# A hybrid retention and attention layer: four orders and one queue changed in its second half

## The chip, the cores and the metric

The kernel runs on one core of one Trainium2 chip, as one launch. The metric is the device time of one execution in microseconds (us). TensorE (PE) multiplies matrices; VectorE (DVE), ScalarE (ACT) and GpSimd (POOL) do elementwise work; transfers are issued by SyncE (SP) or by ScalarE's own queue (ACTq).

## What is computed

One layer over 2048 tokens of width 1024, with 256 context tokens. A modulated RMS norm feeds one projection (3328 columns). Its columns serve two head groups: bidirectional retention (4 heads of 128, chunks of 128 tokens) and windowed attention (8 query heads of 64 on 2 key heads, blocks of 128 tokens, a sink logit, all context keys). Both are gated, joined, projected, added to the input and normed. Cut to what matters here:

```
def step(R, inp):                                   # retention, one chunk of 128 tokens
    qc, kc, vc = inp
    s = jnp.einsum('bhid,bhjd->bhij', qc, kc) * decay_in
    inner = jnp.einsum('bhij,bhje->bhie', s, vc)
    cross = jnp.einsum('bhid,bhde->bhie', qc, R) * decay_q
    R = R * decay_c + jnp.einsum('bhjd,bhje->bhde', kc * decay_k, vc)
    return R, inner + cross
...
y = out_f + jnp.flip(out_b, 2)
y = (y - mu) * lax.rsqrt(var + EPS)                 # per head and token
ret_x = merge_heads(y) * gn_w * jax.nn.silu(g)
...
p = jnp.exp(logits - m); p = p / (jnp.sum(p) + jnp.exp(sink - m))    # attention, 3 blocks + context
att_x = merge_heads(p @ v) * jax.nn.silu(ag)
x = x + gate * (concat([ret_x, att_x]) @ w_out)
return rms_norm(x) * final_norm_w
```

## The kernel before, in words

The first half (to about 677 us) projects all tokens, group by group of 512 tokens (`g` = 3, 2, 1, 0), and stores queries, keys, values, gates and chunk states to DRAM scratch. `do_gate` (L588) applies SiLU to a gate column block and stores it (L595); for the attention gates (`which` = 1) of groups 0 and 1 the store is issued by SP, for all others by ACT. The last attention-gate column block, for group 0, is interleaved on PE with the attention scores of token block 0: `WEAVE` (L35) says after which contraction step `k` of the two column blocks which jobs go. Digits are score heads 0 to 7; `s` is the first block's retention scores and decayed queries; `y` is its retention values, their moments, norm and rows, and its state update (L1127 to L1136).

The second half loops over 16 token blocks `b`, two steps each: `kv` = 0 and 1. In a step, `STEPS[kv]` (L29) lists the order of the calls. `a` is one score head of the next step (`att_head`, L725: four score matmuls into a single buffer S, a DVE operation L749 that adds the mask and takes the maximum, Exp on ACT). `N` divides that head by its sum (`att_norm`, L761: a DVE reciprocal L764 and a POOL scaling L765). `T` transposes one key tile of the four normalised heads on PE (L1155) and splits the result into a high part (ACT, L1157) and a low part (DVE, L1158); `V` multiplies both parts with the values (L1168), one after the other. `o` are pieces of the output projection (L1205). `q` makes the decayed queries of the next block (`ret_queries`, L773: two POOL products, L780), `S` its retention scores, `R` its values (L795 to L799), `B` and `r` its moments, norm and rows (L806 to L821; L814 waits for POOL's inverse root L118), `Y` transposes the rows and makes the gated retention input (L1191, L109, L1194). `U` updates the retention state by four DVE operations (`ret_state`, L823, L828) and issues the load of the next block's states (L686). The tile of decayed queries has one buffer, that of the loaded states two.

The calls are made in this order, but a planner places each instruction on its engine's queue: it goes by the order of the calls and by modelled times, and lets a later instruction that is ready fill a gap. `tc.issue_after(i)` (also as `behind(i)`, L217) makes an instruction stand behind `i` on its engine; it adds an order, no wait on another engine. Each queue then runs in order: an instruction that waits holds up all behind it, and a transfer that waits on SP holds up the transfers behind it.

`last` (L1232) ends the kernel: for each half row, the last output pieces, the addition, a sum of squares on ACT (L1241); then POOL adds the two sums (L1242), adds EPS (L117) and takes the inverse root (L118); then DVE scales both halves (L1245), and SP and ACT store one each.

Of the kernel before, what the change touches and what calls it, by code (L numbers as in the profile page):

```python
# [8 lines left out]
F32 = mybir.dt.float32  # L9
F32R = mybir.dt.float32r  # L10
BF16 = mybir.dt.bfloat16
AF = mybir.ActivationFunctionType
ALU = mybir.AluOpType
# [3 lines left out]
P = 128  # L17
# [6 lines left out]
RH = 4  # L24
AH = 8
EPS = 1e-6
# [5 lines left out]
)  # L32
FIRST = "T0 Y T1 V0 T2 V1 q T3 V2 T4 G V3 S V4"

WEAVE = ("00 21 42 63", "04s 25 46 67y")  # L35
CHUNKS = ["rk0", "rv0", "rk1", "rv1", "rq0", "rq1", "kv", "aq0", "aq1", "rg0", "rg1", "ag0", "ag1"]


# [1 line left out]
def tile_hymba(  # L40
# [17 lines left out]
    nc = tc.nc  # L58
    act, dve, pool, pe = nc.scalar, nc.vector, nc.gpsimd, nc.tensor
# [28 lines left out]
    gC = const.tile([P, 8], F32, name="gC")  # L88
# [4 lines left out]
    half4 = const.tile([P, 4], F32, name="half4")  # L93
# [21 lines left out]
    def inv_sqrt(dst, src, eps):  # L115

        pool.tensor_scalar(dst, src, EPSV[eps], 0.0, op0=ALU.add, op1=ALU.add)  # L117
        pool.tensor_tensor(dst, dst, half4[:, 0 : dst.shape[-1]], op=ALU.pow)  # L118
        return dst
# [10 lines left out]
    def tmp(name, shape=(P, GT), dt=F32):  # L130
        return tp.tile(list(shape), dt, tag="t", name=name)
# [18 lines left out]
    PE = {}  # L150
# [66 lines left out]
    def behind(i):  # L217
        return tc.issue_after(i.ins) if i else nullcontext()
# [369 lines left out]
    def do_gate(which, idx, g, ps, pin=False, t=None):  # L588

        t = tmp(f"g{which}{idx}{g}") if t is None else t  # L590
        i = act.activation(t, ps, AF.Silu)
        if pin:
            tc.keep_in_program_order(i)

        (nc.sync if which and g < 2 else act).dma_start(  # L595
            d_g[4 * g : 4 * g + 4, :, which, idx, :].rearrange("b d t -> d b t"),
            t.rearrange("d (b t) -> d b t", b=4),
        )
# [51 lines left out]
    C2 = {}  # L650

    def window(b):
        slots = sorted((x % 3, x) for x in (b - 1, b, b + 1) if 0 <= x < NB)
        return slots, [x - b + 1 for _, x in slots]
# [8 lines left out]
    VW, QKV, ST, AQ, GR, GA, XB, MR, MA, PB, RF, RT = ({} for _ in range(12))  # L663
# [97 lines left out]
    def att_norm(b, kv, j):  # L761
        n = len(window(b)[0]) * P + CTX
        pb, m4 = PB[(b, kv)]
        dve.reciprocal(m4[:, 2, j : j + 1], m4[:, 2, j : j + 1])  # L764
        pool.tensor_scalar(pb[:, j, 0:n], pb[:, j, 0:n], m4[:, 2, j : j + 1], 0.0, op0=ALU.mult, op1=ALU.add)  # L765

    BANKS = {"o": 1, "z": 2, "t": 3}

    def bank(name, tag="t", shape=(P, RH, P)):
        return (pwr if tag == "o" else pw).tile(list(shape), F32, tag=tag, name=name, bufs=BANKS[tag])  # L770


    def ret_queries(b):  # L773
        if b:
            RT[b] = (
                s1.tile([P, 2, RH, P], F32, tag="qd", name=f"qd{b}", bufs=1),
                s2.tile([P, RH, P], F32, tag="sd", name=f"sd{b}", bufs=1),
            )
        for dr in range(2):
            pool.tensor_tensor(RT[b][0][:, dr], QKV[b][:, 0], C2["decq"][:, dr], op=ALU.mult)  # L780

    def ret_scores(b):
        q, kT = QKV[b][:, 0], QKV[b][:, 1]
# [39 lines left out]
    def ret_state(b):  # L823

        rf, st = RF[b], ST[b]
        nf = st[:, 0] if b else rf
        for h in range(RH):
            dve.scalar_tensor_tensor(  # L828
                nf[:, h], rf[:, h], gC[:, h : h + 1], st[:, 0, h], op0=ALU.mult, op1=ALU.add
            )  # L830
        RF[b + 1] = nf

    def tables():
# [46 lines left out]
    def unit(name, g, w):  # L880
        kind, idx = name[:2], int(name[-1]) if name[-1].isdigit() else 0
        if g == "c":
            {"rk": lambda: ctx_rk(idx, w), "rv": lambda: ctx_rv(idx, w), "kv": lambda: ctx_kv(w)}[kind]()
        elif kind == "rv":
            do_rv(idx, g, w)
        elif kind == "kv":
            do_kv(g, w)
        elif kind in ("rg", "ag"):
            for c in range(2):
                ps = cols_by_tok(w, c * P, H[g], GT, f"{name}{g}{c}")  # L890
                flush()
                do_gate(0 if kind == "rg" else 1, 2 * idx + c, g, ps)
        else:
            finish(name, g, [cols_by_tok(w, c * P, H[g], GT, f"{name}{g}{c}") for c in range(2)])
# [104 lines left out]
    for c in range(4):  # L999
        do_gate(0, c, 3, first[(f"rg{c // 2}", c % 2)])  # L1000
# [27 lines left out]
    for c, ps in enumerate(tiles):  # L1028
        do_gate(0, c, 2, ps)
# [93 lines left out]
    def head(i):  # L1123
        att_head(0, i // 4, i % 4)
        att_norm(0, i // 4, i % 4)
# [7 lines left out]
    ps = []  # L1133
    for c, weave in enumerate(WEAVE):
        at = {int(w[0]): [jobs[x] for x in w[1:]] for w in weave.split()}
# [9 lines left out]
    s2 = ctx.enter_context(tc.tile_pool(name="s2", bufs=2, reuse_waits="tile"))  # L1145
    pw = ctx.enter_context(tc.tile_pool(name="pw", bufs=1, space=PSUM, reuse_waits="tile"))
    fw, vctx = C2["fw"], C2["vctx"]
# [3 lines left out]
    def att_t(b, kv, kt):  # L1151
        pb = PB[(b, kv)][0]
        ppt = bank(f"pt{b}_{kv}_{kt}")
        for j in range(4):
            pe.transpose(ppt[:, j], pb[:, j, kt * P : (kt + 1) * P], ident)  # L1155
        phl = s2.tile([P, 2, 4, P], F32R, tag="phl", name=f"phl{b}_{kv}_{kt}", bufs=2)
        PE["phl"] = act.activation(phl[:, 0], ppt, AF.Copy)  # L1157
        dve.tensor_tensor(phl[:, 1], ppt, phl[:, 0], op=ALU.subtract)  # L1158
        PH[kt] = phl

    def att_v(b, kv, kt):
# [37 lines left out]
    def proj(b, n2, k):  # L1199
        if k == 0:  # L1200
            PZ[n2] = bank(f"pz{b}_{n2}", "z", (P, GT))
        m = (MR if k < RH else MA)[b]
        s = slice(n2 * GT, (n2 + 1) * GT)
        for i, (a, c) in enumerate(PASSES):
            pe.matmul(  # L1205
                PZ[n2], m[:, a, k % RH, :], WG[k // 4][c][:, k % 4, s],
                start=(k == 0 and i == 0), stop=(k == NK - 1 and i == 2),
            )
        if k == NK - 1:
            dve.tensor_tensor(XB[b][:, s], PZ[n2], XB[b][:, s], op=ALU.add)  # L1210
# [21 lines left out]
    def last(b):  # L1232

        xb = XB[b]
        ss = s2.tile([P, 2], F32, tag="sl", name="sl")
        junk = s1.tile([P, D], F32, tag="junk", name="junkl", bufs=1)
        hs = [slice(n * GT, (n + 1) * GT) for n in range(2)]
        for n in range(2):
            for i in range(4):
                proj(b, n, 4 + i)  # L1240
            act.activation(junk[:, hs[n]], xb[:, hs[n]], AF.Square, scale=1.0 / 32, accum_out=ss[:, n : n + 1])  # L1241
        pool.tensor_tensor(ss[:, 0:1], ss[:, 0:1], ss[:, 1:2], op=ALU.add)  # L1242
        rz = inv_sqrt(s2.tile([P, 1], F32, tag="rz", name="rzl"), ss[:, 0:1], 0)
        for n in range(2):
            dve.scalar_tensor_tensor(xb[:, hs[n]], xb[:, hs[n]], rz, fw[:, hs[n]], op0=ALU.mult, op1=ALU.mult)  # L1245
            (act if n else nc.sync).dma_start(out[b * P : (b + 1) * P, hs[n]], xb[:, hs[n]])

    def last_gate():

# [12 lines left out]
    for t in range(2 * NB):  # L1262
        b, kv = t // 2, t % 2
# [142 lines left out]
```

## Time and profile before

| | us |
|---|---|
| three timed runs | 1181.79 (median), 1178.88, 1182.34 |
| the profiled execution, its own time | 1177.99 |
| its span, first to last instruction | 1175.4 |
| PE busy | 1133.2 (96%) |
| DVE, ACT, POOL busy | 798.2, 465.7, 404.5 |

A busy PE includes time in which a matmul waits for its weights, and the second half is a chain of small operations on five queues; so the share of busy time does not say what ends each stretch. That is read from the timeline of a stretch, where an idle time before an instruction stands in brackets with what ended it.

### The profile page before, as it was taken

What the parts mean: (1) busy time and instruction counts of PE and PEld (TensorE: products, weight loads), DVE (VectorE), ACT (ScalarE), POOL (GpSimd) and SP (SyncE); (2) the same over time, 40 slices, a digit from 0 to 9 for tenths busy, and PEclk for the clock granted to TensorE, in tenths of its full rate; (3) what the DMA queues carried; (4) which work ended last, traced back from release to release, by engine and by line L of the source; (5) the groups of instructions that cost most, each with busy time, mean ns of one, the idle gap of its engine ahead of it and who ended that gap; (6) DMA issues with size and microseconds to landing.
All of it is one profiled execution on the core that took longest, in us unless ns stands there. A gap on an engine that the chain in (4) does not pass through costs nothing.

```text
span 1175.4 us, 18111 instructions
## 1 busy us (share of the span) xinstructions
PE 1133.2 (96%) x6290; PEld 973.1 (83%) x6290; DVE 798.2 (68%) x1883; ACT 465.7 (40%) x1025; POOL 404.5 (34%) x517
## 2 busy tenths in 40 slices
PE   7999978999999999999999988999999999999997
PEld 3887857999988889998888877888888888888885
DVE  6974876544783645657666447777777777777774
ACT  3344423432342002331001336555555555555562
POOL 1102654100221200002224335555555555555542
PEclk9998989999999999999999999999999999999999
DMA  8948678542564542533356385444444444444310
GB/s 305 324 152 259 235 228 308 177 132 86 176 215 157 162 125 77 175 119 117 97 162 201 83 210 187 131 130 131 130 130 131 131 130 131 130 130 131 95 37 36
DMA packets 139537, 182.24 MB, mean 155 GB/s; under 512 B 11315, under 2 KB 103091, under 8 KB 139318
## 3 DMA queue, kind: packets, MB, share of 16 engines
q1 hardware_dynamic: 126630, 174.54, 47.3%
q10 hardware_dynamic: 12816, 6.56, 1.8%
q8 instruction: 49, 0.80, 0.3%
q14 instruction: 42, 0.34, 0.1%
HBM read 130.19 MB, written 50.86 MB: 154 GB/s over the span
## 4 chain that ended last, share of the span: by engine, by line
PE 69%; DVE 19%; POOL 3%; ACT 3%; DMA 3%; issue 2%; SPq 1%; DVEq 0%; POOLq 0%; ACTq 0%
PE pz L1205 10%; PE rv L354 8%; PE rk L341 7%; PE aq L341 6%; PE ag L341 6%; PE o L1168 4%; PE rg L341 4%; PE rq L341 4%; PE pt L1155 3%; DVE p L749 3%; DVE phl L1158 3%; PE S L743 3%; PE u L470 2%; PE ak L341 2%; PE S L747 2%
## 5 line engine op out<-in xcount | busy, mean ns | idle before, releaser
L1157 ACT ACTIVATE phl<-pt 128x512 fp32r<-128x512 f32 x156 | 92.7, 595 | 98.8 <-PE pt L1155 96.0
L765 POOL TENSOR_SCALAR p<-p,m 128x640 f32<-128x640 f32 (+1 forms) x128 | 104.1, 814 | 69.9 <-DVE m L764 68.5
L1158 DVE TENSOR_TENSOR phl<-pt,phl 128x512 fp32r<-128x512 f32 x156 | 106.8, 686 | 29.9 <-ACT phl L1157 29.2
L756 ACT ACTIVATE p<-p,m 128x641 f32<-128x641 f32 (+1 forms) x128 | 104.5, 816 | 47.3 <-DVE m L753 47.0
L749 DVE CUSTOM_DVE_ANT_0 p<-S,msk 128x640 f32<-128x640 f32 (+1 forms) x128 | 102.5, 801 | 23.4 <-PE S L747 22.0
L1205 PE MATMUL pz<-wg1h,ma 128*128 128x512 f32 x256 | 106.0, 419 | 0.1
L1205 PE MATMUL pz<-wg0h,mr 128*128 128x512 f32 x256 | 104.0, 409 | 0.6 <-POOL mr L1194 0.4
L1155 PE MATMUL pt<-ident,p 128*128 128x128 f32 x624 | 94.0, 273 | 0.0
L743 PE MATMUL S<-kwin,aq 128*128 128x384 f32 (+1 forms) x256 | 79.2, 332 | 4.2 <-DVE m L749 2.8
L1155 PEld LDWEIGHTS pt<-ident,p 128*128 128x128 f32 x624 | 75.8, 141 | 8.7 <-issue 0.4
L446 ACT ACTIVATE vw<-v,wdec 128x128 fp32r<-128x128 f32 x128 | 43.5, 393 | 80.1 <-DVE v L459 80.1
L747 PE MATMUL S<-kctx,aq 128*128 128x256 f32 x256 | 71.1, 280 | 0.0
L1168 PE MATMUL o<-phl,vwin 128*128 128x512 f32 x184 | 63.1, 422 | 0.8 <-DVE phl L1158 0.6
L743 PEld LDWEIGHTS S<-kwin,aq 128*128 128x128 f32 x256 | 48.0, 188 | 10.7 <-DVE m L749 3.4
L1205 PEld LDWEIGHTS pz<-wg0h,mr 128*128 128x128 f32 x256 | 48.1, 188 | 9.3 <-POOL mr L1194 0.8
L1205 PEld LDWEIGHTS pz<-wg1h,ma 128*128 128x128 f32 x256 | 48.1, 188 | 7.9 <-POOL ma L1183 0.5
L747 PEld LDWEIGHTS S<-kctx,aq 128*128 128x128 f32 x256 | 48.2, 188 | 5.3
L1168 PE MATMUL o<-phl,vctx 128*128 128x512 f32 x128 | 44.7, 414 | 6.8 <-DVE phl L1158 6.7
L1205 PE MATMUL pz<-wg0l,mr 128*128 128x512 f32 x128 | 50.5, 395 | 0.0
L1205 PE MATMUL pz<-wg1l,ma 128*128 128x512 f32 x128 | 50.3, 393 | 0.0
L448 DVE SCALAR_TENSOR_TENSOR vw<-v,wdec,vw 128x128 fp32r<-128x128 f32 x128 | 39.9, 358 | 6.2 <-ACT vw L446 6.2
L780 POOL TENSOR_TENSOR qd<-qkv,decq 128x512 f32<-128x512 f32 x30 | 42.3, 1428 | 1.1
(430 smaller groups left out, 3067.7 us busy)
## 6 DMA issues: line engine op xcount, KB each, us to landing
wss<-in_wss SPq DMA_DIRECT2D x32, 512.0 KB, 6.3
qkv<-d_qkv SPq DMA_DIRECT2D x15, 768.0 KB, 6.2
aq<-d_aq SPq DMA_DIRECT2D x64, 128.0 KB, 3.9
xb<-in_xn SPq DMA_DIRECT2D x16, 512.0 KB, 4.2
out<-xb SPq DMA_DIRECT2D x31, 256.0 KB, 2.3
st<-d_st SPq DMA_DIRECT2D x15, 512.0 KB, 3.8
x<-in_xt SPq DMA_DIRECT2D x12, 512.0 KB, 5.3
xr_x<-in_xn SPq DMA_DIRECT2D x12, 512.0 KB, 3.8
```

What stands on the lines that cost most here:

```text
L341: pe.matmul(ps, w[:, a, k, c0 : c0 + P], ht[b][:, k, :], start=(k == 0 and i == 0), stop=(k == NK - 1 and i == 2),)
L354: pe.matmul(ps, ht[a][:, k, t * P : (t + 1) * P], w[:, b, k, :], start=(k == 0 and i == 0), stop=(k == NK - 1 and i == 2),)
L743: i = pe.matmul(psc[:, o:512].rearrange("p (s t) -> p s t", t=P), AQ[b][:, h, :], C2["kwin"][:, kv, hl, ksel], start=(hl == 0), stop=(hl = ...
L747: pe.matmul(psc[:, 512:768], AQ[b][:, h, :], C2["kctx"][:, kv, hl], start=(hl == 0), stop=(hl == 1))
L749: dve.tensor_tensor_reduce(out=pb[:, j, 0:n], in0=psc[:, o : o + n], in1=mk, op0=ALU.add, op1=ALU.max, scale=1.0, scalar=-3e38, accum_out= ...
L756: act.activation(pb[:, j, 0 : n + 1], pb[:, j, 0 : n + 1], AF.Exp, bias=m4[:, 1, j : j + 1], scale=0.125, accum_out=m4[:, 2, j : j + 1],)
L765: pool.tensor_scalar(pb[:, j, 0:n], pb[:, j, 0:n], m4[:, 2, j : j + 1], 0.0, op0=ALU.mult, op1=ALU.add)
L1155: pe.transpose(ppt[:, j], pb[:, j, kt * P : (kt + 1) * P], ident)
L1157: PE["phl"] = act.activation(phl[:, 0], ppt, AF.Copy)
L1158: dve.tensor_tensor(phl[:, 1], ppt, phl[:, 0], op=ALU.subtract)
L1168: pe.matmul(PO[kv], vt, PH[kt][:, hl], start=(kt == 0 and hl == 0), stop=(kt == nkt - 1 and hl == 1))
L1205: pe.matmul(PZ[n2], m[:, a, k % RH, :], WG[k // 4][c][:, k % 4, s], start=(k == 0 and i == 0), stop=(k == NK - 1 and i == 2),)
```

## The change

Six edits. (1) `WEAVE`: job `y` moves from after head 7 (step 6) to after head 6 (step 4). (2) The attention-gate stores of group 1 go from SP's queue to ACT's. (3) `att_norm` remembers its POOL scaling, and the decayed queries of blocks from 2 on stand behind the last one called before. (4) `att_t` remembers its low part, and the state updates of blocks from 1 on stand behind the last one called before. (5) `last` multiplies each half by the final weights right after its sum of squares, adds EPS to the first sum early, and after the inverse root scales one half on ACT and one on DVE. (6) The two last stores swap queues.

```
-WEAVE = ("00 21 42 63", "04s 25 46 67y")
+WEAVE = ("00 21 42 63", "04s 25 46y 67")
...
-        (nc.sync if which and g < 2 else act).dma_start(
+        (nc.sync if which and g < 1 else act).dma_start(
...
-        pool.tensor_scalar(pb[:, j, 0:n], pb[:, j, 0:n], m4[:, 2, j : j + 1], 0.0, op0=ALU.mult, op1=ALU.add)
+        PE["norm"] = pool.tensor_scalar(
+            pb[:, j, 0:n], pb[:, j, 0:n], m4[:, 2, j : j + 1], 0.0, op0=ALU.mult, op1=ALU.add
+        )
...
-        for dr in range(2):
-            pool.tensor_tensor(RT[b][0][:, dr], QKV[b][:, 0], C2["decq"][:, dr], op=ALU.mult)
+        with behind(PE["norm"] if b > 1 else None):
+            for dr in range(2):
+                pool.tensor_tensor(RT[b][0][:, dr], QKV[b][:, 0], C2["decq"][:, dr], op=ALU.mult)
...
-        for h in range(RH):
-            dve.scalar_tensor_tensor(
-                nf[:, h], rf[:, h], gC[:, h : h + 1], st[:, 0, h], op0=ALU.mult, op1=ALU.add
-            )
+        with behind(PE["low"] if b else None):
+            for h in range(RH):
+                dve.scalar_tensor_tensor(
+                    nf[:, h], rf[:, h], gC[:, h : h + 1], st[:, 0, h], op0=ALU.mult, op1=ALU.add
+                )
...
-        dve.tensor_tensor(phl[:, 1], ppt, phl[:, 0], op=ALU.subtract)
+        PE["low"] = dve.tensor_tensor(phl[:, 1], ppt, phl[:, 0], op=ALU.subtract)
...
+        rz = s2.tile([P, 1], F32, tag="rz", name="rzl")
         hs = [slice(n * GT, (n + 1) * GT) for n in range(2)]
         for n in range(2):
             for i in range(4):
                 proj(b, n, 4 + i)
             act.activation(junk[:, hs[n]], xb[:, hs[n]], AF.Square, scale=1.0 / 32, accum_out=ss[:, n : n + 1])
-        pool.tensor_tensor(ss[:, 0:1], ss[:, 0:1], ss[:, 1:2], op=ALU.add)
-        rz = inv_sqrt(s2.tile([P, 1], F32, tag="rz", name="rzl"), ss[:, 0:1], 0)
+            if n == 0:
+                pool.tensor_scalar(ss[:, 0:1], ss[:, 0:1], EPS, 0.0, op0=ALU.add, op1=ALU.add)
+            dve.tensor_tensor(xb[:, hs[n]], xb[:, hs[n]], fw[:, hs[n]], op=ALU.mult)
+        pool.tensor_tensor(rz, ss[:, 0:1], ss[:, 1:2], op=ALU.add)
+        pool.tensor_tensor(rz, rz, half4[:, 0:1], op=ALU.pow)
+        act.activation(xb[:, hs[0]], xb[:, hs[0]], AF.Copy, scale=rz)
+        dve.tensor_scalar(xb[:, hs[1]], xb[:, hs[1]], rz, None, op0=ALU.mult)
         for n in range(2):
-            dve.scalar_tensor_tensor(xb[:, hs[n]], xb[:, hs[n]], rz, fw[:, hs[n]], op0=ALU.mult, op1=ALU.mult)
-            (act if n else nc.sync).dma_start(out[b * P : (b + 1) * P, hs[n]], xb[:, hs[n]])
+            (nc.sync if n else act).dma_start(out[b * P : (b + 1) * P, hs[n]], xb[:, hs[n]])
```

## Rows read from the trace of the kernel before

**Rows 1.** Windows: stretch; busy us of PE, PEld, DVE, ACT, POOL; clock; DMA

```profile
1065.92:1095.60 29.68, 29.12 (x178) 25.56 (x178) 23.19 (x68) 17.07 (x35) 15.93 (x22) 1.00 0.41 127
1095.60:1124.43 28.83, 28.83 (x178) 25.62 (x178) 22.13 (x64) 17.08 (x35) 15.75 (x22) 1.00 0.30 87
```

**Rows 2.** Waits of PE, 725 us to the end: us in total, times, longest

```profile
PE o L1168 <- DVE phl L1158: 7.3, 13, 0.6
```

**Rows 3.** Timeline of all engines, the stall of one block: start, us, what, [idle before]

```profile
871.68 0.60 ACT L1157 ACTIVATE phl<-pt 128x512 fp32r<-128x512 f32 x1 [0.52 <-PE pt L1155]
...
872.38 0.61 DVE L828 SCALAR_TENSOR_TENSOR st<-st,gC,st 128x128 f32<-128x128 f32 x2
...
872.98 0.60 DVE L828 SCALAR_TENSOR_TENSOR st<-st,gC,st 128x128 f32<-128x128 f32 x2
...
873.16 1.00 POOL L765 TENSOR_SCALAR p<-p,m 128x640 f32<-128x640 f32 x1 [0.90 <-DVE m L764]
873.27 0.40 PE L1168 MATMUL o<-phl,vctx 128*128 128x512 f32 x1
873.49 0.68 DVE L1158 TENSOR_TENSOR phl<-pt,phl 128x512 fp32r<-128x512 f32 x1
...
874.23 0.50 PE L1168 MATMUL o<-phl,vctx 128*128 128x512 f32 x1 [0.56 <-DVE phl L1158]
```

**Rows 4.** Timeline, the same place eight blocks later, with no state update there

```profile
1109.92 0.67 DVE L1158 TENSOR_TENSOR phl<-pt,phl 128x512 fp32r<-128x512 f32 x1
...
1110.74 0.62 PE L1168 MATMUL o<-phl,vctx 128*128 128x512 f32 x2
```

**Rows 5.** Timeline, the step of kv = 0 that follows it

```profile
1116.50 0.69 DVE L1158 TENSOR_TENSOR phl<-pt,phl 128x512 fp32r<-128x512 f32 x1 [0.34 <-ACT phl L1157]
...
1120.54 0.81 POOL L765 TENSOR_SCALAR p<-p,m 128x640 f32<-128x640 f32 x1
...
1121.31 1.31 POOL L1194 TENSOR_TENSOR mr<-gr,mr 128x512 fp32r<-128x512 f32 x1
...
1123.17 0.80 POOL L765 TENSOR_SCALAR p<-p,m 128x640 f32<-128x640 f32 x1 [0.55 <-DVE m L764]
...
1126.79 0.60 PE L1155 MATMUL pt<-ident,p 128*128 128x128 f32 x4
```

**Rows 6.** Timeline of SP's queue, end of the first half

```profile
651.40 16.73 SPq L595 DMA_DIRECT2D d_g<-g  x4
668.19 2.55 SPq L670 DMA_DIRECT2D kwin<-d_k  x4
...
674.65 2.56 SPq L670 DMA_DIRECT2D kwin<-d_k  x4
```

**Rows 7.** Timeline of PE, first score matmul

```profile
679.39 0.39 PE L743 MATMUL S<-kwin,aq 128*128 128x256 f32 x1 [1.45 <-DMA kwin<-d_k]
```

**Rows 8.** Timeline of all engines, the first block's retention rows

```profile
696.74 0.60 ACT L799 ACTIVATE first<-y 128x512 f32<-128x512 f32 x1 [0.61 <-PE y L797]
...
701.42 0.33 PE L1189 MATMUL yt<-ident,first 128*128 128x128 f32 x1 [2.29 <-ACT first L821]
```

**Rows 9.** Timeline of all engines, the state update of block 1

```profile
716.02 4.23 DVE L828 SCALAR_TENSOR_TENSOR st<-sfw,gC,st 128x128 f32<-128x128 f32 x4
...
717.52 2.58 POOL L780 TENSOR_TENSOR qd<-qkv,decq 128x512 f32<-128x512 f32 x2
...
721.50 0.44 PE L743 MATMUL S<-kwin,aq 128*128 128x384 f32 x1 [2.76 <-DVE m L749]
```

**Rows 10.** Timeline of all engines, the end of the kernel

```profile
1168.96 0.63 ACT L1241 ACTIVATE junkl<-xb 128x512 f32<-128x512 f32 x1 [2.01 <-DVE xb L1210]
...
1170.35 0.57 POOL L118 TENSOR_TENSOR rzl<-rzl,half 128x1 f32<-128x1 f32 x1
1170.96 1.42 DVE L1245 SCALAR_TENSOR_TENSOR xb<-xb,rzl,fw 128x512 f32<-128x512 f32 x2 [2.03 <-POOL rzl L118]
...
1172.40 0.38 ACTq L1246 DMA_DIRECT2D out<-xb  x1
```

## The prediction

> **What bounds the kernel now.** I read the windows first. Blocks of the second half follow each other by 29.68 us; in one of them PE has work for 29.12 us, so it is the bound there but for 0.56 us. The block just before the end takes 28.83 us with PE busy throughout, on the same 178 matmuls [rows 1]. So 0.85 us a block is a stall and not work: 0.56 us shown idle, the rest in a matmul stretched by its late start. PE's waits name it: 13 waits, 7.3 us idle in all, all for a low part (DVE, L1158) [rows 2]; 12 of them stand at one place, in the kv = 1 step of 12 blocks running, the 13th near the end in another context.
>
> The timeline of that place shows who is late. ACT has the high part of the last key tile ready at 871.68 + 0.60 = 872.28. But DVE then does four state updates, from 872.38 to 873.5, and only then the low part, 873.49 to 874.17. PE multiplies by the high part at 873.27, would go on 0.23 us later, and starts the low part at 874.23 [rows 3]. Eight blocks later there is no further state to update; there DVE does the low part at 1109.92, it ends at 1110.59, and PE takes both parts back to back from 1110.74 [rows 4]. POOL still makes decayed queries before that place in this block, so the four updates alone cost the 0.85 us; the queries cost nothing there.
>
> The timelines of three other places then show one-time stalls, taken up part by part.
>
> **State behind low parts** (edit 4). In the call order the update follows the second key tile of the kv = 0 step, so the order keeps it behind that tile's low part, which ends at 1117.19 in the same undisturbed block [rows 5]. The stall goes: 12 x 0.85 = 10.2 us. The four updates last 1.1 us together [rows 3] and now stand before the mask operation of head 2 in that step. Behind them wait that operation, the third tile's low part and the product of the retention rows. PE uses that low part only after another tile's transposes, a score head and two output pieces, so a delay near 1 us is covered; were that cover gone, 1 us a block would be lost. The update is also what frees the buffer of the states to be loaded: that load moves into kv = 0 as well, and SP holds what stands behind it that long; its states are read only in the next step, so it should still land in time. Late next on PE in a block: nothing that the trace shows.
>
> Block 1 has the dearest update. It takes 4.23 us instead of 1.1, beside POOL's products, and PE's next score matmul is idle 2.76 us for DVE [rows 9]. The update moves behind block 1's second low part, where POOL has only short work: I take 2.7 us, bounds 0 (another late operation takes the place) and 2.8.
>
> **Decayed queries behind normalisations** (edit 3). 14 blocks, 2.6 to 2.9 us of POOL each [rows 9]. They leave the kv = 1 step, where they cost nothing, and land in kv = 0 behind head 2's scaling. Behind them then waits head 3's scaling, and for it PE's first transposes of the next step. In the undisturbed block head 2's scaling starts at 1120.54, the low half of the retention input takes 1.31 us, and head 3's scaling runs 1123.17 to 1123.97 [rows 5]. With the state update ahead on DVE I let head 2's scaling end 0.6 us later, at 1121.9. Then 1.31 + 2.86 + 0.80 follow without a gap: head 3 ends at about 1126.9. The transposes start at 1126.79, the fourth, which needs head 3, at 0.11 each about 1127.1. So it fits by 0.2 us. I take 0; bounds 0 to 0.5 us a block, 7 us in all. The queries themselves are read only after a second tile's transposes, so they are in time.
>
> **Gate stores on ACT** (edit 2). On SP four stores stand from 651.40 to 668.19, waiting for SiLU; 16 loads of keys, values and queries stand behind them, 0.64 us of issue each (2.55 / 4), and the first score matmul waits for the second set of keys, idle 1.45 us [rows 6, 7]; with the lost slot 1.60. Without the four stores the loads can go out up to 16 us earlier. ACT issues one store in about 0.38 [rows 10]; the stores come 5.6 us apart (16.73 / 3) with one SiLU between, so the four cost nothing there; were ACT full it would be 1.5. Two stores of group 0 stay on SP, ahead of the first block's queries, and those landed just in time, so I take back 0.3: gain 1.3, bounds 0 (the loads' memory is still in use by the last weights) and 1.6.
>
> **Values sooner** (edit 1). PE is idle 2.29 us at the transposes of block 0's retention rows; they wait for ACT, ACT for POOL's root, DVE's moments, and all for the copy of the values at 696.74 [rows 8]. The move puts the 24 value matmuls, their copy, moments, root, rows and four updates ahead of 6 gate matmuls and the four matmuls of head 7: about 1.9 us (6 slots of 0.23, as in [rows 4], and four of half that), and a copy of gate columns that DVE made among the moments comes after them, which may add as much as 0.6. Head 7 itself comes later by the value matmuls and is needed only in the next step. I take 2.3, the whole idle time; bounds 1 and 2.5.
>
> **Last norm** (edits 5 and 6). After the sum of squares [rows 10] the path was three POOL operations and 1.42 us of DVE. Now it is two (0.3 less) and half the scaling on each engine (some 0.7 less): 1.0 to 1.1 us. But the multiplication by the final weights starts as POOL adds the sums. Where DVE and POOL met in this trace one of them lost: the updates of block 1 took fourfold beside POOL, and head 3's scaling 1.00 against 0.80 beside an update [rows 3, 5, 9]. A clash here would cost up to the 0.68 of such an operation. I take 0.6, bounds 0.3 and 1.1. By the rule of the Trainium skill, "SBUF — State Buffer", Who interferes with whom, an instruction of DVE with two SBUF inputs and one of POOL that reads SBUF exclude each other, so the gain would be about 0.5; without that rule it would be 1.1. The updates of block 1 agree with it. The swap of the store queues costs nothing: each follows its own engine or a free one.
>
> **The sum.** 10.2 + 2.7 + 0 + 1.3 + 2.3 + 0.6 = 17.1 us. It is made against the profiled execution, 1178.0, which gives 1160.9. The three timed runs lie 0.9 to 4.4 above that one; the four together have a mean of 1180.2, and against this it is 1163. I take 1163.
>
> **The rivals.**
> 1. Half of the steady gain is given back, by the full POOL queue in kv = 0 (0.2 us of slack is thin) or by DVE's 1.1 us there. For it: POOL is left with no gap of 6 us. Against: the low parts there are used late. 12 x 0.4 = 5 us less: 1168.
> 2. The steady gain does not come, because the planner puts another DVE operation into the gap before the last low part, or puts the update where it holds up another low part. For it: DVE waits there for POOL's root, and the planner fills such gaps. Against: in the block without an update nothing else filled it [rows 4]. Only 6.9 us of the one-time gains stay: 1173.
> 3. Slower: the decayed queries hold head 3's scaling past the fourth transpose in every block. It decides from 1127.1 on; each us beyond it costs 14 us. To lose all 17 it must end 1.2 us later than that, at 1128.3, which needs the queries stretched by half or head 2's scaling 1.4 us later than I let it. For it: 2.6 to 2.9 us is the longest POOL work of a block. Against: no such stretch stands in the trace. With 1.5 us: 14 x 1.5 - 17 = 4 slower, 1184.
> 4. The order changes nothing, because the planner had these instructions behind such operations already. Against: the update stands in kv = 1 in the trace, a step ahead of its call. The one-time edits would still act, so this ends with rival 2.
>
> **How the numbers follow.** A difference under 0.3%, 3.5 us, can hardly be told from none. My forecast has 0.6, its own range 1160 to 1167. Rival 1 has 0.17, rivals 2 and 4 together 0.12, rival 3 has 0.11, of which 0.06 slower by over 0.3% and 0.05 about as before. Faster by over 0.3% come the first three, 0.6 + 0.17 + 0.12 = 0.89, less 0.02 for one-time gains that fail along with the steady one: 0.87; the same 0.07, slower 0.06. The low end has all upper bounds, 10.2 + 2.8 + 1.6 + 2.5 + 1.1 = 18.2, from the profiled execution: 1159.8, so 1159. The high end takes in rival 1 and most of rivals 2 and 4: 1173.
>
> **What would show it.** Right: blocks follow by 28.8 us; the four updates stand after a second low part in kv = 0 and the last low part of kv = 1 directly after L814; PE's wait for low parts shrinks from 13 to about one; the first score matmul shows no wait for keys, no 2.3 us before the retention rows' transposes, no 2.8 us in block 1; the last store is issued 0.6 us sooner after the last matmul. Wrong: a PE wait for L765 at the first transposes of kv = 1 (rival 3, or 1 if short), blocks still near 29.7 with DVE busy before the last low part (rival 2), the keys' loads still issued after 668 us (edit 2), or a state load that PE waits for.

## The result, and the profile after

The changed kernel takes 1163.65 us in the median of five runs (1162.40 to 1166.40), the kernel before 1181.79 (1178.88 to 1182.34, five runs); the ratio is 0.9865, with a 95% interval of 0.9846 to 0.9883. That is 16.8 us between the means of the runs (1180.8 and 1164.0), 14 to 18 by the interval. The forecast was 1163. The profiled execution took 1162.40, its span is 1160.6 (before: 1177.99 and 1175.4).

First the window of one block of the second half, from the changed kernel. It answers to [rows 1]; the columns are the same.

```profile
849.85:878.68 28.83, 28.83 (x178) 25.63 (x176) 22.89 (x68) 17.19 (x35) 15.44 (x23) 1.00 0.45 135
```

Blocks follow by 28.83 us instead of 29.68, and PE is busy throughout: the 0.85 us is gone from every block. PE's waits in the second half answer to [rows 2] (us in total, times, longest):

```profile
PE s L790 <- DMA first<-d_qkv: 1.7, 1, 1.7
PE o L1172 <- DVE phl L1162: 1.0, 3, 0.6
PE pz L1209 <- POOL mr L109: 0.8, 1, 0.8
PE pz L1209 <- POOL mr L1198: 0.4, 1, 0.4
PE o L1172 <- ACT phl L1161: 0.4, 1, 0.4
PE yt L1193 <- DVE glast L1142: 0.2, 1, 0.2
```

The 13 waits for a low part have become 3 (of the 1.0 us, 0.6 is the one near the end that was there before). The waits for keys, the long one for the first block's rows and the one for block 1's mask are gone. New is a wait of 1.7 us for the first block's queries; and the short waits just behind the first block's rows, three of 0.8 us in sum before (for ACT and POOL), are five of 2.1 us now. The timeline of one block shows where the updates and the decayed queries stand now; it answers to [rows 3 and 5]:

```profile
864.17 0.16 DVE L817 SCALAR_TENSOR_TENSOR ra<-mv,ra 128x4 f32<-128x4 f32 x1 [1.50 <-POOL ra L118]
...
864.32 0.67 DVE L1162 TENSOR_TENSOR phl<-pt,phl 128x512 fp32r<-128x512 f32 x1
865.15 0.63 PE L1172 MATMUL o<-phl,vctx 128*128 128x512 f32 x2
...
870.91 0.69 DVE L1162 TENSOR_TENSOR phl<-pt,phl 128x512 fp32r<-128x512 f32 x1 [0.34 <-ACT phl L1161]
871.52 1.13 DVE L832 SCALAR_TENSOR_TENSOR st<-st,gC,st 128x128 f32<-128x128 f32 x4
872.57 0.82 DVE L749 CUSTOM_DVE_ANT_0 p<-S,msk 128x640 f32<-128x640 f32 x1
...
875.57 1.31 POOL L1198 TENSOR_TENSOR mr<-gr,mr 128x512 fp32r<-128x512 f32 x1
876.85 0.81 POOL L765 TENSOR_SCALAR p<-p,m 128x640 f32<-128x640 f32 x1
877.61 2.54 POOL L783 TENSOR_TENSOR qd<-qkv,decq 128x512 f32<-128x512 f32 x2
880.12 0.82 POOL L765 TENSOR_SCALAR p<-p,m 128x640 f32<-128x640 f32 x1
...
881.32 0.60 PE L1159 MATMUL pt<-ident,p 128*128 128x128 f32 x4
```

In kv = 1 DVE goes from the moments' last operation (L817) and one small reciprocal (L764, at 864.25) to the last low part, and PE's two matmuls at 865.15 show no idle time. In kv = 0 the updates follow the second low part. On POOL, head 2's scaling, the queries and head 3's scaling follow one another without a gap; the last ends at 880.94, 0.38 us ahead of the first transpose of the next step and some 0.7 ahead of the fourth, which needs it.

The start of the second half answers to [rows 6 to 8]:

```profile
667.40 1.28 ACT L880 ACT_TABLE_LOAD   x1 [0.48 <-ACT g L591]
...
671.39 2.56 SPq L670 DMA_DIRECT2D kwin<-d_k  x4
676.12 2.07 SPq L595 DMA_DIRECT2D d_g<-g  x2
678.28 0.59 SPq L698 DMA_DIRECT2D first<-d_qkv  x1
...
677.00 0.28 PE L743 MATMUL S<-kwin,aq 128*128 128x256 f32 x1
687.03 1.16 PE L790 MATMUL s<-first 128*128 128x128 f32 x8 [1.73 <-DMA first<-d_qkv]
699.02 1.26 PE L1193 MATMUL yt<-ident,first 128*128 128x128 f32 x4 [0.15 <-DVE glast L1142]
701.13 0.49 PE L1172 MATMUL o<-phl,vwin 128*128 128x512 f32 x1 [0.42 <-ACT phl L1161]
...
706.86 0.50 PE L1209 MATMUL pz<-wg0h,mr 128*128 128x512 f32 x1 [0.81 <-POOL mr L109]
708.21 0.73 PE L1209 MATMUL pz<-wg0h,mr 128*128 128x512 f32 x2 [0.45 <-POOL mr L1198]
```

The second set of keys goes out at 671.39, three us sooner, and the first score matmul no longer waits. It does not go out sooner still: the first set now does, at 642.05, but loads between the two wait on SP for the landing of gate stores, which ACT issues now (SP's waits, 642 to 690 us):

```profile
SPq L706 <- DMA d_g<-g: 15.3, 3, 5.1
```

And the queries that follow the keys land 8.75 us after their issue (678.28 to 687.03), and PE waits 1.73 us for them. One idle time of 2.29 us ahead of the rows' transposes has become one of 0.15, with five short ones behind it (two of 0.23 us for low parts, at 701.86 and 704.21, stand between those shown). The six make 2.29 us again; what edit 1 gains is taken up at the run no_values. The end of the kernel answers to [rows 10]:

```profile
1154.94 0.69 DVE L1249 TENSOR_TENSOR xb<-xb,fw 128x512 f32<-128x512 f32 x1 [0.79 <-ACT junkl L1246]
1155.06 0.63 POOL L1250 TENSOR_TENSOR rzl<-sl 128x1 f32<-128x1 f32 x1 [2.05 <-ACT junkl L1246]
...
1156.37 0.72 ACT L1252 ACTIVATE xb<-xb,rzl 128x512 f32<-128x512 f32 x1 [1.46 <-POOL rzl L1251]
1156.37 0.49 DVE L1253 TENSOR_SCALAR xb<-xb,rzl 128x512 f32<-128x512 f32 x1 [0.74 <-POOL rzl L1251]
1156.88 0.33 SPq L1255 DMA_DIRECT2D out<-xb  x1
1157.12 0.38 ACTq L1255 DMA_DIRECT2D out<-xb  x1
```

POOL's sum of two numbers a row lasts as long as DVE's multiplication beside it: both end near 1155.65.

**A table by stage.** One or two us are little beside the spread of the runs, so the experiments are read from marks within each profile. Time 0 is ScalarE's table load at the end of the first half (667.40 above; 667.77 before), so that what differs between executions of the first half stays out. Marks on PE, each at the start of a matmul: the first score matmul; the first block's retention score product, *s(0)*; that of the third block, *s(2)*; then the length from s(2) to the product of the last block, *s(15)*, thirteen blocks later; the length from there to the last matmul of the output projection (`pz`); from that to the end of the span; and the end.

| kernel | first score | s(0) | s(2) | s(2) to s(15) | to last pz | to the end | end |
|---|---|---|---|---|---|---|---|
| before | 11.62 | 19.61 | 71.50 | 385.00 | 43.54 | 7.63 | 507.67 |
| changed | 9.60 | 19.63 | 67.11 | 374.84 | 43.69 | 7.58 | 493.22 |
| state_only | 11.27 | 19.29 | 68.49 | 374.86 | 43.55 | 7.63 | 494.53 |
| no_state | 9.60 | 19.49 | 66.96 | 384.98 | 43.57 | 7.58 | 503.09 |
| no_queries | 9.60 | 18.90 | 66.37 | 374.83 | 43.51 | 7.57 | 492.27 |
| queries_only | 11.39 | 19.74 | 69.82 | 385.12 | 43.56 | 7.64 | 506.15 |
| all_stores_act | 9.60 | 20.81 | 68.09 | 374.83 | 43.79 | 7.58 | 494.30 |
| no_stores | 11.28 | 19.90 | 67.36 | 374.84 | 43.75 | 7.58 | 493.53 |
| no_values | 9.60 | 17.89 | 67.14 | 374.83 | 43.77 | 7.58 | 493.32 |
| old_tail | 9.60 | 18.69 | 66.17 | 374.83 | 43.77 | 7.64 | 492.40 |
| more_pool | 9.60 | 19.84 | 67.30 | 383.47 | 45.01 | 7.58 | 503.36 |
| later_apart | 9.60 | 19.63 | 65.13 | 374.83 | 43.78 | 7.40 | 491.14 |

Where two kernels have the same stage, its length repeats within 0.4 us, that of the steady stretch within 0.14 and that of the end within 0.01; s(0) does not repeat, which is one of the findings.

### The profile page after: what moved, and what is told of

The parts are those of the page before. It is cut to its first block, busy times and chain, and to the rows that moved or that the text cites. A ratio compares the mean times of both kernels' runs of the same rounds, so it can differ in the third digit from the quotient of the medians.

```text
span 1160.6 us, 18086 instructions
## 1 busy us (share of the span) xinstructions
PE 1130.3 (97%) x6290; PEld 974.3 (84%) x6290; DVE 792.4 (68%) x1884; ACT 467.8 (40%) x1026; POOL 399.9 (34%) x517
## 4 chain that ended last, share of the span: by engine, by line
PE 80%; DVE 9%; DMA 4%; POOL 2%; ACT 2%; issue 2%; SPq 0%; POOLq 0%; DVEq 0%; ACTq 0%
PE pz L1209 14%; PE rv L354 8%; PE rk L341 8%; PE ag L341 6%; PE o L1172 6%; PE pt L1159 5%; PE aq L341 5%; PE rg L341 4%; PE rq L341 4%; PE S L743 3%; PE S L747 2%; PE u L470 2%; PE ak L341 2%; DVE wss L215 2%; PE av L341 1%
## 5 line engine op out<-in xcount | busy, mean ns | idle before, releaser
L1183 DVE TENSOR_TENSOR mf<-o,ob 64x256 f32<-64x256 f32 x64 | 26.7, 417 | 24.6 <-ACT ob L1180 23.9
L1172 PE MATMUL o<-phl,vctx 128*128 128x512 f32 x128 | 41.4, 403 | 0.2 <-DVE phl L1162 0.2
```

What stands on the lines that cost most here:

```text
L1172: pe.matmul(PO[kv], vt, PH[kt][:, hl], start=(kt == 0 and hl == 0), stop=(kt == nkt - 1 and hl == 1))
```

## The experiments

**state_only.** The kernel before with edit 4 alone.

```
+        with behind(PE["low"] if b else None):
             for h in range(RH):
...
+        PE["low"] = dve.tensor_tensor(phl[:, 1], ppt, phl[:, 0], op=ALU.subtract)
```

> The kernel before with edit 4 alone: the four state updates stand behind a second low part. My theory (the updates ahead of the last low part are the whole steady stall): blocks of the second half follow by 28.8 us instead of 29.68, no PE wait for a last low part in 12 blocks, block 1's 2.76 us wait gone, so 10.2 + 2.7 = 12.9 us less than before, about 1168, and the other marks as before (first score matmul near 679 with its 1.45 us wait for keys, 2.3 us before the retention rows' transposes). Rival (the move of the queries is part of it, because POOL's products hold DVE's work back in kv = 1): blocks follow by more than 29.0 us and the low part waits for something else there; then 5 us less or fewer, 1174 or above.

Measured: 1166.03 us, ratio 0.9895 (0.9881 to 0.991), some 12.4 us less. The steady stretch is 374.86 instead of 385.00, and from the second block's score product to the third's it takes 24.74 us instead of 27.43: 10.14 and 2.69 us. PE still waits for keys (1.1 us) and ahead of the rows' transposes (2.3 us), and no longer for block 1's mask. Edit 4 alone is three quarters of the result, at both its prices.

**no_state.** The changed kernel without edit 4.

```
-        with behind(PE["low"] if b else None):
-            for h in range(RH):
+        for h in range(RH):
```

> The changed kernel without edit 4: the updates go back to where the planner had them. My theory: the stall at the last low part is back in 12 blocks, they follow by about 29.7 us, and the time is 10 us or more above the changed kernel, 1174 to 1177. Rival (moving the decayed queries out of kv = 1 is enough, or the planner now puts the updates elsewhere): blocks follow by 28.8 to 29.0 us and the time stays within 3 us of the changed kernel.

Measured: 1172.98 us, ratio 0.9947 (0.9932 to 0.9963), 9.3 above the changed kernel, a little under the expected span's lower end. Its waits of PE, and the window of one block:

```profile
PE o L1171 <- DVE phl L1161: 7.6, 15, 0.6
```

```profile
823.00:852.68 29.68, 29.12 (x179) 25.56 (x177) 23.18 (x69) 17.05 (x35) 15.54 (x23) 1.00 0.41 129
```

The stall is back, with the very numbers of [rows 1 and 2]: 29.68 us a block, PE at work 29.12. So moving the queries gives none of the steady gain. But block 1's long wait is not back; queries_only says why.

**no_queries.** The changed kernel without edit 3.

```
-        with behind(PE["norm"] if b > 1 else None):
-            for dr in range(2):
+        for dr in range(2):
```

> The changed kernel without edit 3: decayed queries back in the kv = 1 step. My theory (they cost nothing there once the updates have left): blocks follow by 28.83 us and the time is that of the changed kernel within 1 us, 1163 to 1164. Rival (edit 3 is needed, because POOL's products there meet DVE's low part or the root that DVE waits for): blocks follow by 29.1 us or more, 1167 or above.

Measured: 1162.18 us, ratio 0.9862 (0.9847 to 0.9878). The steady stretch is 374.83, as in the changed kernel. Edit 3 is worth nothing once the others are there.

**queries_only.** The kernel before with edit 3 alone.

```
+        with behind(PE["norm"] if b > 1 else None):
+            for dr in range(2):
```

> The kernel before with edit 3 alone. My theory: the updates still stand ahead of the last low part, so blocks follow by about 29.7 us and the time is that of before within 3 us; only block 1's updates, which took 4.23 us beside POOL's products, no longer meet them, so a part of the 2.76 us there may go. Rival (the queries made the stall): blocks follow by 28.8 to 29.0 us, 1170 or below.

Measured: 1176.11 us, ratio 0.9975 (0.9963 to 0.9988), 2.7 less. The steady stretch stays at 385.12; block 1 takes 25.53 us instead of 27.43. Its timeline there, against [rows 9]:

```profile
717.37 0.73 POOL L1186 TENSOR_TENSOR ma<-mf,ma 128x256 fp32r<-128x256 f32 x1
717.38 2.20 DVE L831 SCALAR_TENSOR_TENSOR st<-sfw,gC,st 128x128 f32<-128x128 f32 x4
718.08 0.84 POOL L765 TENSOR_SCALAR p<-p,m 128x640 f32<-128x640 f32 x1
720.84 0.44 PE L743 MATMUL S<-kwin,aq 128*128 128x384 f32 x1 [0.87 <-DVE m L749]
```

With the queries' 2.58 us gone from beside them, block 1's four updates take 2.20 us instead of 4.23, and PE's wait is 0.87 instead of 2.76. Two POOL operations still stand beside them. In the changed kernel POOL is idle meanwhile, and they take 1.13:

```profile
727.38 1.13 DVE L832 SCALAR_TENSOR_TENSOR st<-sfw,gC,st 128x128 f32<-128x128 f32 x4
```

So 4.23, 2.20 and 1.13 us for the same four instructions, by what POOL does meanwhile. Block 1's 2.69 us go through edit 4 alone, and 1.9 of them through edit 3 alone: the two do not add. In the Trainium skill, "SBUF — State Buffer", Who interferes with whom, a DVE instruction with two SBUF inputs and a POOL instruction that reads SBUF exclude each other; these three lengths agree. In no_state, with edits 1 and 3 and without edit 4, the updates take 2.12 us and PE shows no wait in block 1 either.

**all_stores_act.** The changed kernel with the two gate stores of group 0 on ACT's queue too.

```
-        (nc.sync if which and g < 1 else act).dma_start(
+        act.dma_start(
```

> The changed kernel with the two gate stores of group 0 on ScalarE's queue too, so that none stands on SP ahead of the first block's queries. Theory A (these queries land late because SP issues them late, behind two stores at 676.12): their load is issued some 4 us sooner, PE's 1.73 us wait at the first score product goes, and the first score product of the first block comes 1.5 to 1.8 us sooner after the first score matmul; nothing else changes, 1162 at best, which the times hardly tell from the changed kernel. Theory B (they land late because the keys, values and queries share the transfer engines): the load is issued sooner, takes longer, and 1 us or more of the wait stays.

Measured: 1164.62 us, ratio 0.9874 (0.9852 to 0.9895); s(0) 1.2 us later, with a wait of 2.5. Neither theory was put to the test, since the queries' load did not go out sooner. SP's queue:

```profile
672.21 8.79 SPq L670 DMA_DIRECT2D kwin<-d_k  x4
683.17 0.38 SPq L698 DMA_DIRECT2D first<-d_qkv  x1
```

```profile
SPq L670 <- DMA d_g<-g: 6.3, 1, 6.3
```

The four loads of keys now wait 6.3 us for the landing of a gate's store, which ACT issues only at 678.07, behind the start of its last SiLU, and everything behind them on SP waits too: the queries go out four us later, not sooner. They land 5.85 us after their issue, where it was 8.75 in the changed kernel: issued later, they travel for a shorter time. Whether the two stores are in the queries' way stays open, and why these keys wait for that store here and not in the changed kernel was not tried.

**no_stores.** The changed kernel without edit 2 (`g < 2` again).

```
-        (nc.sync if which and g < 1 else act).dma_start(
+        (nc.sync if which and g < 2 else act).dma_start(
```

> The changed kernel without edit 2: all four gate stores on SP again. If edit 2 gave 1.6 us at the first score matmul and lost 1.7 at the first block's queries, as the two traces suggest: PE's wait for keys of about 1.4 us is back, the wait of 1.7 us for queries goes, the stretch from the first score matmul to the first score product is 8.0 us instead of 10.0, and the end stands within 0.5 us of the changed kernel. If the prediction's 1.3 us was right and the queries' wait comes from elsewhere: the end is 1.3 us later, with both waits.

Measured: 1163.74 us, ratio 0.9867 (0.9847 to 0.9888). PE waits 1.1 us for keys and 0.4 for queries; the first score matmul is 1.68 us later, s(0) 0.27 later, the end 0.31 later. So in this pair edit 2 is worth 0.3 us. Over all profiles: with the four stores on SP (before, state_only, queries_only, no_stores) s(0) stands at 19.29 to 19.90, mean 19.64; with two on ACT (changed, no_state, no_queries, no_values, old_tail, more_pool) at 17.89 to 19.84, mean 19.07. The first score matmul gains 1.67 to 2.02 us every time. But the queries, issued 1.75 us sooner, land 7.0 to 9.0 us after their issue where before they took 7.3 at most, and that gives back between nothing and the whole. The six kernels have SP's queue in the same order there, so the difference among them is not an edit but the transfers' own; with a spread of 2 us, the mean of six is itself good to some 0.3 us. From 676 to 688 us, in the changed kernel's trace, the queue's packets take 98.4% of the sixteen engines' time (packets, MB, share):

```profile
q1 hardware_dynamic: 2605, 3.01, 98.4%
```

In the kernel before they take as much at the same place (105.9%, 676.4 to 688.4 us; packets are counted where they start). Engines that are full in either order would let a load land at about the same time however early it is issued; that is my reading, and no run has emptied them.

**no_values.** The changed kernel without edit 1.

```
-WEAVE = ("00 21 42 63", "04s 25 46y 67")
+WEAVE = ("00 21 42 63", "04s 25 46 67y")
```

> The changed kernel without edit 1: the first block's values after the gates and heads again. If the prediction's 2.3 us stands: the wait of 2.3 us ahead of the retention rows' transposes is back, and the stretch from the first score product to that of block 1 is 24.4 to 24.6 us instead of 23.3, with the small waits behind it (pz for mr 0.8 and 0.4, o 0.4) gone, so net 1.2 of the 2.3. Rival: those small waits stay, they belong to something else, and the loss is the whole 2.3.

Measured: 1163.84 us, ratio 0.9875 (0.9849 to 0.9901). The queries happened to land in time here, so the end says nothing; from s(0) to s(2) it takes 49.25 us where the changed kernel takes 47.48. Edit 1 is worth 1.77 us. (The stretch that the expectation named, to the second block's score product, is 24.51 against 23.32; but with edit 1 four matmuls fewer fall behind that product, so the mark itself has moved, and only the longer stretch counts.) The wait is back at the rows' transposes:

```profile
699.89 0.33 PE L1193 MATMUL yt<-ident,first 128*128 128x128 f32 x1 [2.29 <-ACT first L824]
```

The windows from s(0) to s(2), here and in the changed kernel, and a stretch of the first:

```profile
685.78:735.03 49.25, 46.95 (x266) 39.65 (x266) 31.49 (x101) 27.21 (x55) 24.10 (x31) 0.93 0.56 172
```

```profile
687.03:734.51 47.48, 45.04 (x264) 37.88 (x265) 30.91 (x97) 26.82 (x53) 24.17 (x31) 1.00 0.58 178
```

```profile
700.77:707.60 6.83, 6.82 (x19) 4.65 (x20) 3.90 (x6) 3.71 (x7) 1.75 (x3) 0.50 0.77 279
```

PE's idle time is 2.30 us in the first window (49.25 - 46.95) and 2.44 in the second: edit 1 has split it and not removed it. What is shorter is the time in which PE is busy, by 1.9 us on the same matmuls, and the rows show one reason for that: without edit 1 the granted clock is 0.50 for 6.83 us behind the wait, with it 1.00 throughout. Yet the slow clock may have hidden other waits. The kernel before, in which it lasts 3.41 us, takes as long from s(0) to the second block's product (24.46 us against 24.51), with PE 1.0 us less at work and 0.9 more idle, most of it for ACT and POOL. So how much of the 1.77 us comes from the clock, and how much from an earlier start of the work behind the transposes, was not separated. The transposes come 2.12 us sooner after s(0) (14.11 against 11.99), and 1.77 of these last.

**old_tail.** The changed kernel without edits 5 and 6: the last norm and its store queues as in the kernel before.

```
-        pool.tensor_tensor(rz, rz, half4[:, 0:1], op=ALU.pow)
-        act.activation(xb[:, hs[0]], xb[:, hs[0]], AF.Copy, scale=rz)
-        dve.tensor_scalar(xb[:, hs[1]], xb[:, hs[1]], rz, None, op0=ALU.mult)
...
+        rz = inv_sqrt(s2.tile([P, 1], F32, tag="rz", name="rzl"), ss[:, 0:1], 0)
...
+            dve.scalar_tensor_tensor(xb[:, hs[n]], xb[:, hs[n]], rz, fw[:, hs[n]], op0=ALU.mult, op1=ALU.mult)
```

> The changed kernel without edits 5 and 6: the last norm as before. If the prediction's 0.6 us stands: the end comes 0.6 us later after the last matmul. If both stores share the transfer engines, so that only the bytes after the first issue count, as the two traces suggest: the first store is issued within 0.1 us and the last 0.5 us later, and the end comes 0.0 to 0.2 us later after the last matmul.

Measured: 1163.87 us, ratio 0.9868 (0.9846 to 0.989). From the last matmul to the end it takes 7.64 us against 7.58. Over all profiles the four with the old tail have 7.63 or 7.64, the seven with the new one 7.57 or 7.58: 0.06 us. Edits 5 and 6 were not taken apart.

**more_pool.** The changed kernel with one more POOL product behind the decayed queries.

```
             for dr in range(2):
                 pool.tensor_tensor(RT[b][0][:, dr], QKV[b][:, 0], C2["decq"][:, dr], op=ALU.mult)
+            if b > 1:
+                pool.tensor_tensor(RT[b][0][:, 0], QKV[b][:, 0], C2["decq"][:, 0], op=ALU.mult)
```

> The changed kernel with one more product of decayed queries on POOL in blocks 2 to 15 (about 1.3 us, the first product done twice), in the place where edit 3 has put them, ahead of head 3's scaling. It prices rival 3, the slack behind edit 3. In the changed kernel's trace head 3's scaling ends about 0.4 us before the step's first transposes and 0.7 us before the fourth one. If that slack is all there is: PE waits for head 3's scaling in each block, 1.3 - 0.7 = 0.6 us a block, blocks follow by 29.4 us instead of 28.83, about 8 us more in all, 1171 to 1173. If there is none (PE is already held there): 1.3 us a block, 18 us more. If the planner or another gap takes it up: blocks follow by 28.83 us and the time stays within 2 us of the changed kernel.

Measured: 1172.53 us, ratio 0.9932 (0.9906 to 0.9958). Blocks follow by 29.50 us, 0.67 more, and the end is 10.1 us later. PE's waits:

```profile
PE pt L1161 <- POOL p L765: 6.1, 14, 0.5
```

POOL's queue in one block:

```profile
883.32 2.54 POOL L783 TENSOR_TENSOR qd<-qkv,decq 128x512 f32<-128x512 f32 x2
885.81 1.31 POOL L785 TENSOR_TENSOR qd<-qkv,decq 128x512 f32<-128x512 f32 x1
887.08 0.83 POOL L765 TENSOR_SCALAR p<-p,m 128x640 f32<-128x640 f32 x1
```

Head 3's scaling starts 1.27 us later (885.81 to 887.08), 0.67 of it reaches PE in each of 14 blocks: the slack behind edit 3 is 0.6 us. The mechanism of the slower rival is real, and the change stays 0.6 us a block short of it.

**later_apart.** The changed kernel with two edits of my own.

```
-WEAVE = ("00 21 42 63", "04s 25 46y 67")
+WEAVE = ("00 21 42 63", "04 25s 46y 67")
...
-            dve.tensor_tensor(xb[:, hs[n]], xb[:, hs[n]], fw[:, hs[n]], op=ALU.mult)
+                dve.tensor_tensor(xb[:, hs[n]], xb[:, hs[n]], fw[:, hs[n]], op=ALU.mult)
...
-        dve.tensor_scalar(xb[:, hs[1]], xb[:, hs[1]], rz, None, op0=ALU.mult)
+        dve.scalar_tensor_tensor(xb[:, hs[1]], xb[:, hs[1]], rz, fw[:, hs[1]], op0=ALU.mult, op1=ALU.mult)
```

> The changed kernel with two edits of my own, a whole slot later for the first block's score product (behind the next 8 gate matmuls, 1.86 us) and a last norm in which the second half is multiplied by the root and the weights in one operation, so that DVE has no work beside POOL's sum. First: the queries' landing has taken 7.0 to 8.75 us from its issue in the runs so far, against 5.8 to the product, so the wait of 0 to 1.73 us goes and the second block of the steady stretch starts 66.0 us or less after the end of the first half's last table load, against 67.1 in the changed kernel's trace and 66.2 to 67.1 in its variants. If something behind the product sets the pace instead (its mask, its own values), the wait only moves, and it stays at 66.2 to 67.1. Second: POOL's sum takes 0.19 us instead of 0.63, both stores go out 0.2 to 0.4 us sooner, and the end comes 0.2 to 0.4 us sooner after the last matmul (7.2 to 7.4 us instead of 7.56); if the end hangs on the transfer alone, 0.1 or less. Both together 1 to 2 us under the changed kernel, 1162, too little for the times to tell for sure.

Measured: 1161.97 us, ratio 0.9849 (0.9826 to 0.9872), the lowest median of all. PE shows no wait for the queries, though the product comes 8.74 us after their issue; s(2) stands at 65.13, two us ahead of the changed kernel's and one ahead of the best of its variants. From the last matmul to the end it takes 7.40 us:

```profile
1154.12 0.19 POOL L1250 TENSOR_TENSOR rzl<-sl 128x1 f32<-128x1 f32 x1 [2.07 <-ACT junkl L1246]
...
1155.00 0.75 DVE L1253 SCALAR_TENSOR_TENSOR xb<-xb,rzl,fw 128x512 f32<-128x512 f32 x1 [1.78 <-POOL rzl L1251]
1155.75 0.41 ACTq L1255 DMA_DIRECT2D out<-xb  x1
1155.78 0.33 SPq L1255 DMA_DIRECT2D out<-xb  x1
```

POOL's sum takes 0.19 us again, so its 0.63 was the clash with DVE's multiplication. The first store goes out 3.65 us after the last `pz` matmul (1152.10) where it was 3.84, the second 3.68 where it was 4.08; the end gains 0.18. It follows the first store (0.19), not the second (0.40). By the marks it ends 2.1 us ahead of the changed kernel; the medians, measured apart, differ by 1.7, which the intervals cannot tell from none.

## Why the prediction was right, and where its terms were off

- **State behind low parts, steady part.** 10.2 predicted; 10.16 in the changed kernel and 10.14 with edit 4 alone. Both sides were shown, with it and without it. The cover in kv = 0 held: no PE wait behind the updates there. Rivals 2 and 4 fell with it: the planner put nothing else into the gap.
- **Block 1's update.** 2.7 predicted, 2.69 measured. That the update is dear because of POOL was right too; edit 3 would have had 1.9 of it by itself, and edits 1 and 3 the whole, which the prediction did not see, and which costs its sum nothing.
- **Decayed queries.** 0 predicted, 0 measured, with slack of 0.6 us where I had 0.2. The planner took another order than mine: it put the low half of the retention input (875.57) ahead of head 2's scaling instead of behind it, and the queries took 2.54 us instead of 2.86. Rival 3 priced its mechanism rightly (0.67 us a block for 1.27 us more of POOL work), and rival 1 had no place either, since nothing is late in kv = 0.
- **Gate stores.** 1.3 predicted, 0.6 measured on the mean, near nothing in the profiled execution. The step that failed is the 0.3 us taken back for the first block's queries. The first score matmul did gain even more than the 1.6; but the queries "landed just in time" before, and I let them keep their travel time. Issued sooner, they took up to 9.0 us, and PE waited up to 1.9 us there. A wait of one load had been traded for that of the next. That the loads can go out up to 16 us earlier held for the first set of keys only (642.05 against 668.19). The second, for which PE waits, went out three us sooner, still after 668, which was one of my signs of being wrong: loads ahead of it wait for the landing of gate stores (15.3 us in the row above). The first score matmul needed no more than that.
- **Values sooner.** 2.3 predicted, 1.77 measured, and not by the mechanism that I had. The step that failed is to take the idle time as gain. It did not go: 0.15 stays, for the copy that I had named as the risk (`glast`, L1142), and 2.14 came back in five short waits for what is late next, attention's high and low parts and POOL's retention input. What became shorter is PE's busy time, by 1.9 us, next to a granted clock that no longer falls to 0.50 behind the wait; the prediction had no term for the clock. That 1.77 is as near to 2.3 as it is was partly luck.
- **Last norm.** 0.6 predicted, 0.06 measured. The path did shorten, and the clash was as feared: POOL's sum 0.63 us instead of 0.19. The last store is issued 0.51 us sooner after the last matmul (4.08 against 4.59). The step that failed is to count that as the end. The end stands 3.7 us behind the issue of the first store with all three tails (7.63 - 3.92, 7.58 - 3.84, 7.40 - 3.65), and 3.0 to 3.7 behind that of the second; and the first store left only 0.08 us sooner (3.84 against 3.92). That the second half's transfer has to follow the first's, because they share the engines, is my reading of it.

The measured terms make 10.15 + 2.69 + 0 + 0.6 + 1.77 + 0.06 = 15.3 us against 17.1; the means of the timed runs differ by 16.8, with an interval of 14 to 18, which holds both. The kernel before, timed again beside the experiments, had means of 1179.2, 1179.7 and 1180.0 us where it was 1180.8 here; against those the changed kernel gains 15.2 to 16.0. So the forecast's closeness is partly luck: three small terms were 1.8 us too large together, and the two that carry it, three quarters of the sum, were right to 0.1.

## What to carry to other kernels

A stall that repeats by the block is worth reading to the hundredth: compare a block that has it with one that does not, name the operation in between, and the price is exact. One-time stalls are not: each gain there is the distance to what is late next, so look for the next load's landing, the next engine's short wait, or the first of two stores that share the transfer engines, before taking the whole idle time as gain, and look at the granted clock behind it: an idle time can be split without getting less, and the time still fall. And where an operation is moved into a full queue, measure the slack by putting more in: here 0.6 us a block lay between no cost and 14 times the excess.

## What the runs showed of the hardware that I had not expected

- **The clock after an idle time.** In no_values PE idles 2.29 us ahead of the transposes, to 699.89, and from 700.77 to 707.60 its granted clock is 0.50, the level of 1.2 GHz. In state_only and queries_only the same idle time is followed by the same 6.83 us at that level, in the kernel before by 3.41:

```profile
702.79:706.20 3.41, 3.26 (x10) 2.22 (x10) 1.39 (x3) 1.30 (x3) 0.00 (x0) 0.50 0.64 195
```

In the eight kernels with edit 1 the waits at that place make up as much (0.15 + 0.42 + 0.23 + 0.23 + 0.81 + 0.45 = 2.29 in the changed kernel), none over 0.81, and leave the clock at 1.00 to the end of PE's work. Yet an idle time as long is not always followed by a fall: block 1's 2.76 us in the kernel before and the 2.51 us ahead of s(0) in all_stores_act were followed by a clock of 1.00. And twice the slow time did not lengthen the stretch: from the transposes to the second block's score product it takes 10.42 us before and 10.40 in no_values. What it would take with no slow time and no edit 1 was not tried.
- **A tiny operation can be held as long as a large one.** POOL's sum of 128 x 1 took 0.63 us beside DVE's 128 x 512, and 0.19 without.
- **A landing time has a spread of its own.** The same 768 KB load, in the same place of the same queue, landed between at most 7.0 and 9.0 us after its issue, and 5.85 us after it where it was issued four us later (all_stores_act).
